# Up-projection loads counted as longer in the planner, and the down-projection's token blocks finished in turn

## The chip, the cores and the metric

One core of one Trainium2 chip. The metric is the device time of one execution, in microseconds (us); of the kernel before three executions were timed. One execution was profiled besides; all rows below are from it.

## What is computed

One decoder layer in float32 on 1024 tokens of width 1024 (token mixing, then a squared-ReLU MLP). The change touches the MLP only, the last line of the reference:

```python
h = rms_norm(x, g_ffn_norm[l])
x = x + jnp.square(jax.nn.relu(h @ w_up[l])) @ w_down[l]   # w_up 1024 x 4096, w_down 4096 x 1024
```

## The kernel before

**Recording and planning.** The kernel does not emit instructions directly. Every call records a node in a `Plan` (so all of them stand at line 268, and the profile tells them apart by the names of their tiles). `Plan.schedule` (line 340) then decides the order of the instructions on every engine by playing the program through with costs of its own (`cost`, line 292): whenever an engine is free it takes, of the nodes that are ready in this play, the one with the highest `prio`, and that order is issued. An engine executes its instructions in that order, so a wait of one holds up all that stand behind it. Two numbers matter here. `n.prio` (line 376) is the longest chain of work behind a node, less 0.03 per place in the recorded program, plus `plus`. `done` (line 454) is when the node's result is there for others; for a DMA it is

```python
line = max(t + .4, line) + n.bytes / .36e6
done = line + 1.75
```

**Precision.** Each float32 operand is split in two float32r tiles: ScalarE (ACT) copies the high part, VectorE (DVE) or GpSimd (POOL) subtracts it from the original for the low part (`split`, line 1455). `mm3` makes three TensorE (PE) matmuls of 128x512 for each product.

**Up-projection** (`up_raw` line 1444, `product` 1469, `pair` 1539): 16 pairs of 128-column blocks of `w_up`. For each pair a load of 1 MB on SP's queue fills a tile `wu` (three buffers in turn), eight ACT instructions scale it by the norm's gain, POOL makes sums of it (`s1` to `s4`), and seven products of 12 matmuls follow (a Strassen-Winograd form). Their operand `we` is split from `wu` or from an `s`; there are six buffers for it. The products go into PSUM banks `X`, `Z`, `W`. `Z` takes the product S1, is copied out to a tile `d` by ACT, and then has S4 added to it, so PE's first matmul of S4 (`Z<-B22h`) waits for that copy (`d<-Z`). DVE and POOL combine the results, and SP stores them to DRAM (`u_d`).

**Down-projection** (line 1640): eight chunks `c` of two pairs, each with seven parts `p`. A part reads `u_d` (`ur`, split to `uu`) and the rows of `w_down` (`wd`, combined by POOL to `T`, split to `we`), and makes 4 token blocks `j` x 2 pairs x 3 = 24 matmuls into four banks, one for each `j`. After each block's six matmuls DVE adds the bank to the output rows `y` (`tt(nc.vector, y, X[j], y, ALU.add)`, line 1674). Parts 0 to 3 accumulate in the same four banks `X`, so the next part's first matmul into a bank waits for the add of the part before; parts 4 and 5, and part 6, use banks `Z`. In the last chunk the adds of parts 3 to 6 are followed by stores to the output.

Of the kernel before, what the change touches and what calls it, by code (L numbers as in the profile page):

```python
# [150 lines left out]
class Plan:  # L151
# [73 lines left out]
    done = False  # L225
# [8 lines left out]
    def op(self, name, engine, method, a, kw):  # L234
        views = [("" if i else "out", v) for i, v in enumerate(a)] + list(kw.items())
        views = [(k, v) for k, v in views if isinstance(v, View)]
        preds, raw, touched = set(), set(), []
        for k, v in views:
            w = k in ("out", "accum_out")
            r0, r1, m = v.region()  # L240
            touched.append((v.base, w, r0, r1, m))
            assert v.base.pool.bases is not None, v.base.kw
            preds.add(v.base.node.k)
            for n, ow, o0, o1, om in v.base.seen:
                if (w or ow) and r0 < o1 and o0 < r1 and m & om:
                    preds.add(n.k)
                    if ow:
                        raw.add(n.k)
        out = views[0][1] if views else None
        if name == "PE":  # L250
            preds.update([n.k for n in out.base.nodes if n.engine == "PE"][-1:])
        last = self.last_pe if name == "PE" else None
        if (last is not None and last.out is out.base and len(last.do) < self.GROUP and method == "matmul" and
                all(p <= last.k for p in preds)):
            node = last
            preds.discard(node.k)
        else:
            node = self.node(name)
            node.out = out.base if out is not None else None
        node.preds |= preds  # L260
        node.raw |= raw
        node.preds.update(p.k for p in self.follow)
        if name == "PE":
            self.last_pe = node

        def real(x):
            return x.real() if isinstance(x, View) else x
        node.do.append(lambda: getattr(engine, method)(*[real(x) for x in a], **{k: real(x) for k, x in kw.items()}))  # L268
        for b, w, r0, r1, m in touched:
            if b not in node.bases:  # L270
                b.nodes.append(node)
                node.bases.append(b)
            if w:
                b.seen = [s for s in b.seen if not (r0 <= s[2] and s[3] <= r1 and s[4] & ~m == 0)]
            b.seen.append((node, w, r0, r1, m))
        busy, late, size = self.cost(name, method, a, kw, views)
        node.plus = self.plus
        node.late = node.busy + late
        node.busy += busy
        node.port = self.port  # L280
        node.bytes += size
        node.names = method + " " + " ".join(v.base.kw["name"] for _, v in views)
        return node
# [1 line left out]
    last_pe = None  # L285
    plus = 0.0
    follow = ()
    drag = 1.0
    LINK = .05
    GROUP = 1  # L290

# [48 lines left out]
    def schedule(self, weight=lambda n: -.03 * n.k, rings=True):  # L340
# [52 lines left out]
        while True:  # L393
            while stack:
                n = stack.pop()
# [29 lines left out]
            n = nodes[heapq.heappop(ready[e])[1]]  # L425
# [29 lines left out]
            done = t + hold + n.late  # L455
            if n.bytes:
                line = max(t + .4, line) + n.bytes / .36e6
                done = line + 1.75
                if e != "POOL":
                    landed.append(done + .05)  # L460
            end = max(end, done)
            order.append(n)
            for b in n.bases:
# [32 lines left out]
def trunk_layer(ctx, tc, x, g_mix_norm, w_in, g_q, g_k, pe_cmp, w_cmp1, b_cmp1, w_cmp2, b_cmp2,  # L496
                conv_w, g_out, w_o, g_ffn_norm, w_up, w_down, out):
    plan = Plan(tc)
# [16 lines left out]
    def tt(eng, o, a, b, op):  # L515
        eng.tensor_tensor(o, a, b, op=op)

    def copy_act(o, i, scale=1.0):
        nc.scalar.activation(o, i, AF.Copy, scale=scale)
# [376 lines left out]
    with ExitStack() as b2:  # L896
# [150 lines left out]
        def y_tile(shape, name):  # L1047
            return yp.tile(shape, F32, name=name, tag="y", bufs=6)
# [164 lines left out]
        for it, tb in [*enumerate(ORDER)][6:] + [*enumerate(ORDER)][:6]:  # L1213
# [3 lines left out]
            for nh in range(2):  # L1217
                n = slice(nh * 512, (nh + 1) * 512)
# [25 lines left out]
    with ExitStack() as c_:  # L1244
# [112 lines left out]
        done = []  # L1357
# [49 lines left out]
        def bank_p(name):  # L1407
            return psP.tile([P, 512], F32, name=name, tag="pt")
# [35 lines left out]
        def up_raw(q):  # L1444
            raw = (ex.tile([P, KD, 2 * P], F32, name="wu", tag="x") if q % 3 == 0 else
                   vp.tile([P, KD, 2 * P], F32, name="wu", tag=("vs", "vw")[q % 3 - 1]))
            nc.sync.dma_start(raw, wuv[:, :, q * 2 * P:(q + 1) * 2 * P])
            for k in range(KD):
                copy_act(raw[:, k], raw[:, k], scale=cols[:, G_FFN + k:G_FFN + k + 1])
            return {f"A{i + 1}{j + 1}": raw[:, 4 * j:4 * j + 4, i * P:(i + 1) * P] for i in range(2) for j in range(2)}  # L1450

        def w_unit():
            return [ew.tile([P, 512], F32R, name="we", tag=f"w{q}", bufs=6) for q in "hl"]

        def split(pair, raw, eng):
            hi, lo = pair
            copy_act(hi, raw)
            tt(eng, lo, raw, hi.bitcast(F32), ALU.subtract)
            return hi, lo
# [53 lines left out]
    def bank_1(name):  # L1513
        return psD.tile([P, 512], F32, name=name, tag="1", bufs=1)

    def temp(name):
        return eT.tile([P, 512], F32, name=name, tag="t", bufs=4)
# [102 lines left out]
    def down_raw(q):  # L1620
        raw = (vp.tile([P, 2, D], F32, name="wd", tag=("vs", "vw")[q % 2]) if q % 4 < 2 else
               eR.tile([P, 2, D], F32, name="wd", bufs=2))
        nc.sync.dma_start(raw, wdv[:, 2 * q:2 * q + 2])
        B = {f"B{j + 1}{n + 1}": raw[:, j, n * 512:(n + 1) * 512] for j in range(2) for n in range(2)}
        B["T3"], B["T2"] = [temp(n) for n in ("T3", "T2")]
        tt(nc.gpsimd, B["T3"], B["B22"], B["B12"], ALU.subtract)
        return B

    def down_comb(B, name):
        if name == "T2":  # L1630
            B["T1"] = B["B12"]
            tt(nc.gpsimd, B["T1"], B["B12"], B["B11"], ALU.subtract)
            tt(nc.gpsimd, B["T2"], B["B22"], B["T1"], ALU.subtract)
        if name == "T4":
            B["T4"] = B["T2"]
            tt(nc.gpsimd, B["T4"], B["B21"], B["T2"], ALU.subtract)
        return B[name]

    ACC = [(0, 0), (0, 1), (1, 1), (1, 0), (1, 1), (0, 1), (0, 0)]
    for c in range(NPAIR // CHUNK):  # L1640
        qs = range(c * CHUNK, (c + 1) * CHUNK)
        Bs = [down_raw(q) for q in qs]
        if c == 0:
            for tb in [th * 4 + j for th in TH for j in range(4)]:
                yacc[tb] = ey.tile([P, D], F32, name=f"y{tb}")
        X = [None] * 4
        for p in range(7):
            ops = []
            for i, q in enumerate(qs):
                if c == 0 and p < 2:  # L1650
                    both = (y_tile([P, 2, 512], "uf") if p else (yl, e1)[i].tile([P, 2, 512], F32, name="uf", tag="x")).bitcast(F32R)
                    u, ur = [both[:, 0], both[:, 1]], both[:, 1].bitcast(F32)
                else:
                    u = [eU.tile([P, 512], F32R, name="uu", tag=f"u{h}", bufs=10) for h in "hl"]
                    ur = eu.tile([P, 512], F32, name="ur", bufs=8)
                nc.sync.dma_start(ur, u_d[q][p])
                split(u, ur, nc.gpsimd if i else nc.vector)
                w = split(w_unit(), down_comb(Bs[i], WANT[p]), nc.vector if i else nc.gpsimd)
                ops.append((u, w))
            if c == 0 and p in (0, 1):  # L1660
                for tb in range(TH[p] * 4, TH[p] * 4 + 4):
                    nc.sync.dma_start(yacc[tb], x2_d[tb * P:(tb + 1) * P])
            ih, n = ACC[p]
            for j in range(4):
                if p == 0:
                    X[j] = bank_p("X") if j < 3 else bank_1("X")
                elif p in (4, 6):
                    X[j] = bank_d("Z") if j % 2 else bank_e("Z")
                t = slice(j * P, (j + 1) * P)
                for i, ((uh, ul), (wh, wl)) in enumerate(ops):  # L1670
                    mm3(X[j], uh[:, t], ul[:, t], wh, wl, i == 0 and p in (0, 4, 6), i == CHUNK - 1, skip_group_check=True)
                tb = TH[ih] * 4 + j
                y = yacc[tb][:, n * 512:(n + 1) * 512]
                tt(nc.vector, y, X[j], y, ALU.add)
                if c == NPAIR // CHUNK - 1 and p >= 3:
                    nc.sync.dma_start(out2d[tb * P:(tb + 1) * P, n * 512:(n + 1) * 512], y)
    plan.issue()
# [28 lines left out]
```

## Time and profile before

| | us |
|---|---|
| median of 3 executions (lowest, highest) | 1235.27 (1233.68, 1236.08) |
| the profiled execution's own time | 1237.24 |
| its span, first to last instruction | 1235.5 |
| PE busy in the span | 1206.5 (98%) |
| DVE, ACT, POOL busy | 933.4, 713.5, 702.5 |
| up-projection in steady state | about 640 to 880 |
| down-projection | about 919 to 1235 |

In the rows, times are us unless ns is written; a row of a timeline has its start, its length, engine, line, operation, output<-inputs, shapes, how often, and in brackets the idle time before it and what ended that. The ends of PE's matmuls are modelled and overlap the next one's start, so what a wait costs PE is read from the starts. SPq is SP's sequencer, the queue that issues the DMAs.

### The profile page before, as it was taken

The page shows a single profiled execution, that of the slowest core. Times are in us where ns is not written, and L with a number is a line of the kernel's source. Part 1 is how long each engine was busy: PE and PEld are TensorE (multiplying, and loading weights), DVE is VectorE, ACT ScalarE, POOL GpSimd, SP SyncE. Part 2 cuts the span into 40 slices and gives each one's busy share as a digit, 9 for nine tenths or more (in the row PEclk, how much of TensorE's full clock was granted, in tenths as well). Part 3 has the DMA queues.
Part 4 walks back from the last instruction along what each step waited for, and adds up shares of the span by engine and source line. Part 5 has one row for each costly group of instructions (what it writes and reads, how often), then busy time and mean ns, then how long its engine had stood idle before and what let it go on. Part 6 is the DMA issues. An engine that isn't in the chain of part 4 may idle for free.

```text
span 1235.5 us, 18345 instructions
## 1 busy us (share of the span) xinstructions
PE 1206.5 (98%) x5970; PEld 994.5 (80%) x5970; DVE 933.4 (76%) x1784; ACT 713.5 (58%) x1586; POOL 702.5 (57%) x629
## 2 busy tenths in 40 slices
PE   7999999999989999999999999999999999999998
PEld 6878977777878888888788888788887787888786
DVE  6968857683787889988875656566668998888874
ACT  7567855551678888778865555545345444444440
POOL 2544300011245545335878777777889999888860
PEclk9999999999999999999999999999999999999999
DMA  6265621263110100002235453534549544553413
GB/s 244 60 192 192 169 72 51 69 216 141 61 69 35 69 17 20 27 18 75 80 131 167 148 179 123 164 117 161 186 146 393 182 148 162 166 168 130 129 39 136
DMA packets 104215, 156.06 MB, mean 126 GB/s; under 512 B 20212, under 2 KB 58184, under 8 KB 104120
## 3 DMA queue, kind: packets, MB, share of 16 engines
q1 hardware_dynamic: 97976, 147.09, 35.8%
q10 hardware_dynamic: 5376, 5.24, 1.2%
q0 software_dynamic: 768, 2.56, 0.7%
q8 instruction: 47, 0.77, 0.2%
q14 instruction: 48, 0.39, 0.1%
HBM read 106.63 MB, written 48.23 MB: 125 GB/s over the span
## 4 chain that ended last, share of the span: by engine, by line
PE 80%; DVE 6%; DMA 4%; ACT 3%; issue 2%; POOL 1%; SPq 0%; DVEq 0%; ACTq 0%; POOLq 0%
PE X L268 24%; PE Z L268 16%; PE zX L268 5%; PE tp L268 5%; PE ot L268 4%; PE wa L268 4%; PE W L268 4%; PE zp L268 3%; PE wc L268 3%; DMA wu<-in_w_up_dram 3%; PE zZ L268 3%; PE zW L268 1%; DVE y L268 1%; DVE we L268 1%; PE hp L268 1%
## 5 line engine op out<-in xcount | busy, mean ns | idle before, releaser
L268 PE MATMUL X<-we,uu 128*128 128x512 f32 x720 | 179.5, 390 | 2.0 <-DVE y L268 1.8
L268 PEld LDWEIGHTS X<-we,uu 128*128 128x128 f32 x720 | 134.5, 188 | 32.2 <-ACT uu L268 3.0
L268 PE MATMUL Z<-we,uu 128*128 128x512 f32 x576 | 146.8, 391 | 0.4 <-DVE y L268 0.4
L268 ACT ACTIVATE uu<-ur 128x512 fp32r<-128x512 f32 x108 | 66.7, 630 | 123.6 <-PE X L268 58.1
L268 PEld LDWEIGHTS Z<-we,uu 128*128 128x128 f32 x576 | 107.3, 188 | 25.4 <-DVE y L268 2.2
L268 ACT ACTIVATE pt<-pt,nm 128x640 f32<-128x640 f32 (+7 forms) x128 | 93.9, 737 | 25.5 <-DVE nm L268 24.8
L268 PE MATMUL tp<-ident,pt 128*128 128x128 f32 x528 | 103.3, 273 | 1.3 <-DVE pl L268 1.0
L268 POOL TENSOR_TENSOR d<-d 128x512 f32<-128x512 f32 x64 | 98.1, 1553 | 10.2 <-DVE d L268 8.2
L268 ACT ACTIVATE ph<-tp 128x512 fp32r<-128x512 f32 (+1 forms) x148 | 82.1, 575 | 31.2 <-PE tp L268 28.8
L268 DVE TENSOR_TENSOR pl<-tp,ph 128x512 fp32r<-128x512 f32 (+1 forms) x148 | 94.7, 655 | 7.2 <-ACT ph L268 6.7
L268 DVE TENSOR_TENSOR y<-X,y 128x512 f32<-128x512 f32 x128 | 79.8, 681 | 13.9 <-PE X L268 13.1
L268 POOL TENSOR_TENSOR uu<-ur,uu 128x512 fp32r<-128x512 f32 x54 | 77.5, 1438 | 13.8 <-DVE y L268 8.7
L268 DVE TENSOR_TENSOR we<-s,we 128x512 fp32r<-128x512 f32 x42 | 39.4, 937 | 56.6 <-ACT we L268 27.0
L268 DVE TENSOR_TENSOR uu<-ur,uu 128x512 fp32r<-128x512 f32 x54 | 71.2, 1331 | 12.9 <-ACT uu L268 12.3
L268 PEld LDWEIGHTS tp<-ident,pt 128*128 128x128 f32 x528 | 68.6, 140 | 13.8 <-POOL pt L268 1.4
L268 DVE TENSOR_TENSOR y<-Z,y 128x512 f32<-128x512 f32 x96 | 61.3, 683 | 20.3 <-PE Z L268 20.3
L268 ACT ACTIVATE wu<-wu,cols 128x256 f32<-128x256 f32 x128 | 55.6, 500 | 24.0 <-DMA wu<-in_w_up_dram 23.1
L268 ACT ACTIVATE we<-wu 128x512 fp32r<-128x512 f32 x57 | 35.9, 631 | 57.5 <-PE X L268 48.6
L268 DVE SCALAR_TENSOR_TENSOR d<-d 128x512 f32<-128x512 f32 x48 | 68.2, 1423 | 0.8
L268 ACT ACTIVATE we<-s 128x512 fp32r<-128x512 f32 x55 | 34.4, 626 | 49.8 <-PE Z L268 30.2
L268 POOL IOTA d_sw<- 128x640 f32 (+1 forms) x2 | 1.2, 610 | 109.0 <-PE zZ L268 109.0
L268 PE MATMUL zp<-w_lo,hTh 128*128 128x512 f32 (+1 forms) x192 | 62.4, 365 | 0.1
(1334 smaller groups left out, 3714.4 us busy)
## 6 DMA issues: line engine op xcount, KB each, us to landing
u_d<-d SPq DMA_DIRECT2D x112, 256.0 KB, 4.1
ur<-u_d SPq DMA_DIRECT2D x108, 256.0 KB, 2.8
wu<-in_w_up_dram SPq DMA_DIRECT2D x16, 1024.0 KB, 5.5
wd<-in_w_down_dram SPq DMA_DIRECT2D x16, 1024.0 KB, 5.8
xt<-in_x_dram SPq DMA_DIRECT2D x10, 512.0 KB, 4.8
w_raw<-in_w_in_dram SPq DMA_DIRECT2D x8, 512.0 KB, 5.4
w_raw<-in_w_cmp_dram SPq DMA_DIRECT2D x16, 256.0 KB, 2.7
q_d<-qn SPq DMA_DIRECT2D x8, 512.0 KB, 3.4
```

The source lines that it names most:

```text
L268: node.do.append(lambda: getattr(engine, method)(*[real(x) for x in a], **{k: real(x) for k, x in kw.items()}))
```

## The change

Nodes get a number `slack`, which the play adds to `done` of a DMA. The loads of `w_up` for the pairs from 3 on get 5 us of it (`up_raw`); the other loads that are named get 0. In the down-projection the matmuls and the add of token block `j` get a `plus` of 0.7 x (3 - j). No instruction is added or removed, and none computes anything else.

```diff
--- before.py
+++ after.py
@@ -274,7 +274,7 @@
                 b.seen = [s for s in b.seen if not (r0 <= s[2] and s[3] <= r1 and s[4] & ~m == 0)]
             b.seen.append((node, w, r0, r1, m))
         busy, late, size = self.cost(name, method, a, kw, views)
-        node.plus = self.plus
+        node.plus, node.slack = self.plus, self.slack
         node.late = node.busy + late
         node.busy += busy
         node.port = self.port
@@ -285,7 +285,7 @@
     last_pe = None
     plus = 0.0
     follow = ()
-    drag = 1.0
+    drag, slack = 1.0, 0.0
     LINK = .05
     GROUP = 1
 
@@ -458,6 +458,7 @@
                 done = line + 1.75
                 if e != "POOL":
                     landed.append(done + .05)
+                done += n.slack
             end = max(end, done)
             order.append(n)
             for b in n.bases:
@@ -1444,7 +1445,9 @@
         def up_raw(q):
             raw = (ex.tile([P, KD, 2 * P], F32, name="wu", tag="x") if q % 3 == 0 else
                    vp.tile([P, KD, 2 * P], F32, name="wu", tag=("vs", "vw")[q % 3 - 1]))
+            plan.slack = 5.0 if q > 2 else 0.0
             nc.sync.dma_start(raw, wuv[:, :, q * 2 * P:(q + 1) * 2 * P])
+            plan.slack = 0.0
             for k in range(KD):
                 copy_act(raw[:, k], raw[:, k], scale=cols[:, G_FFN + k:G_FFN + k + 1])
             return {f"A{i + 1}{j + 1}": raw[:, 4 * j:4 * j + 4, i * P:(i + 1) * P] for i in range(2) for j in range(2)}
@@ -1620,7 +1623,9 @@
     def down_raw(q):
         raw = (vp.tile([P, 2, D], F32, name="wd", tag=("vs", "vw")[q % 2]) if q % 4 < 2 else
                eR.tile([P, 2, D], F32, name="wd", bufs=2))
+        plan.slack = float(0)
         nc.sync.dma_start(raw, wdv[:, 2 * q:2 * q + 2])
+        plan.slack = 0.0
         B = {f"B{j + 1}{n + 1}": raw[:, j, n * 512:(n + 1) * 512] for j in range(2) for n in range(2)}
         B["T3"], B["T2"] = [temp(n) for n in ("T3", "T2")]
         tt(nc.gpsimd, B["T3"], B["B22"], B["B12"], ALU.subtract)
@@ -1653,7 +1658,9 @@
                 else:
                     u = [eU.tile([P, 512], F32R, name="uu", tag=f"u{h}", bufs=10) for h in "hl"]
                     ur = eu.tile([P, 512], F32, name="ur", bufs=8)
+                plan.slack = 0.0
                 nc.sync.dma_start(ur, u_d[q][p])
+                plan.slack = 0.0
                 split(u, ur, nc.gpsimd if i else nc.vector)
                 w = split(w_unit(), down_comb(Bs[i], WANT[p]), nc.vector if i else nc.gpsimd)
                 ops.append((u, w))
@@ -1667,11 +1674,13 @@
                 elif p in (4, 6):
                     X[j] = bank_d("Z") if j % 2 else bank_e("Z")
                 t = slice(j * P, (j + 1) * P)
+                plan.plus = float(.7) * (3 - j) if True else 0.0
                 for i, ((uh, ul), (wh, wl)) in enumerate(ops):
                     mm3(X[j], uh[:, t], ul[:, t], wh, wl, i == 0 and p in (0, 4, 6), i == CHUNK - 1, skip_group_check=True)
                 tb = TH[ih] * 4 + j
                 y = yacc[tb][:, n * 512:(n + 1) * 512]
                 tt(nc.vector, y, X[j], y, ALU.add)
+                plan.plus = 0.0
                 if c == NPAIR // CHUNK - 1 and p >= 3:
                     nc.sync.dma_start(out2d[tb * P:(tb + 1) * P, n * 512:(n + 1) * 512], y)
     plan.issue()
```

**ACT, up-projection, the load `wu_8788`** (in the profiled execution the one issued at 770.50). `we` are high parts, `d` are results copied out of PSUM; `wu<-wu,cols` scales the load's pieces. Before:

```order
L268 ACTIVATE we_8821<-wu_8470 128x512
L268 ACTIVATE d_8675<-X_8468 128x512
L268 ACTIVATE wu_8788<-wu_8788,cols_64 128x256
L268 ACTIVATE we_8845<-s2_8715 128x512
L268 ACTIVATE d_8690<-Z_8613 128x512
L268 ACTIVATE wu_8788<-wu_8788,cols_64 128x256 x6
L268 ACTIVATE we_8877<-s1_8711 128x512
L268 ACTIVATE d_8840<-X_8654 128x512
L268 ACTIVATE we_8890<-s3_8752 128x512
L268 ACTIVATE wu_8788<-wu_8788,cols_64 128x256
L268 ACTIVATE we_8913<-s4_8773 128x512
```

Now:

```order
L268 ACTIVATE we_8821<-wu_8477 128x512
L268 ACTIVATE d_8671<-X_8468 128x512
L268 ACTIVATE we_8845<-s2_8709 128x512
L268 ACTIVATE d_8686<-Z_8612 128x512
L268 ACTIVATE we_8871<-s1_8703 128x512
L268 ACTIVATE d_8840<-X_8656 128x512
L268 ACTIVATE we_8883<-s3_8749 128x512
L268 ACTIVATE wu_8788<-wu_8788,cols_64 128x256 x7
L268 ACTIVATE we_8912<-s4_8773 128x512
L268 ACTIVATE wu_8788<-wu_8788,cols_64 128x256
```

All eight scalings of the load now stand behind the copy `d<-Z`, the copy `d<-X` and three high parts; before, one stood ahead of these and six more ahead of three of them.

**DVE, down-projection, end of part 0 of the sixth chunk.** `y` are the output rows, X the banks of the four token blocks; `uu` and `we` are low parts. Before:

```order
L268 TENSOR_TENSOR we_11908<-T3_11592,we_11918 128x512
L268 TENSOR_TENSOR uu_11946<-ur_11743,uu_11939 128x512
L268 TENSOR_TENSOR y0_10044<-X_11799,y0_10044 128x512
L268 TENSOR_TENSOR y1_10043<-X_11807,y1_10043 128x512
L268 TENSOR_TENSOR y2_10042<-X_11813,y2_10042 128x512
L268 TENSOR_TENSOR y3_10041<-X_11820,y3_10041 128x512
L268 TENSOR_TENSOR we_11962<-T2_11621,we_11968 128x512
```

Now:

```order
L268 TENSOR_TENSOR y2_10042<-Z_11852,y2_10042 128x512
L268 TENSOR_TENSOR y0_10044<-X_11750,y0_10044 128x512
L268 TENSOR_TENSOR y3_10041<-Z_11870,y3_10041 128x512
L268 TENSOR_TENSOR we_11923<-T3_11610,we_11931 128x512
L268 TENSOR_TENSOR y1_10043<-X_11773,y1_10043 128x512
L268 TENSOR_TENSOR y2_10042<-X_11806,y2_10042 128x512
L268 TENSOR_TENSOR y3_10041<-X_11825,y3_10041 128x512
L268 TENSOR_TENSOR uu_11953<-ur_11758,uu_11946 128x512
```

The add of block 0 has moved ahead of a low part, and the four adds stand no longer in one run.

**PE, the same place.** Before, from the last matmul of part 0 into block 0's bank, X_11799, to the next part's:

```order
L268 MATMUL X_11799<-we_11804,uu_11707 128x512
L268 MATMUL X_11813<-we_11795,uu_11701 128x512
L268 MATMUL X_11807<-we_11804,uu_11707 128x512
L268 MATMUL X_11820<-we_11795,uu_11701 128x512
L268 MATMUL X_11813<-we_11804,uu_11707 128x512
L268 MATMUL X_11820<-we_11804,uu_11707 128x512
L268 MATMUL X_11799<-we_11836,uu_11720 128x512
L268 MATMUL X_11799<-we_11826,uu_11720 128x512
```

Now, from the last matmul of part 0 into block 0's bank, X_11750; the next part's first into it is the fourth row below these:

```order
L268 MATMUL X_11750<-we_11812,uu_11707 128x512
L268 MATMUL X_11773<-we_11812,uu_11700 128x512
L268 MATMUL X_11806<-we_11775,uu_11681 128x512
L268 MATMUL Z_11870<-we_11783,uu_11652 128x512
L268 MATMUL X_11773<-we_11803,uu_11700 128x512
L268 MATMUL X_11806<-we_11787,uu_11688 128x512
L268 MATMUL X_11825<-we_11787,uu_11681 128x512
L268 MATMUL X_11773<-we_11812,uu_11707 128x512
L268 MATMUL X_11806<-we_11812,uu_11700 128x512
L268 MATMUL X_11825<-we_11775,uu_11681 128x512
L268 MATMUL X_11806<-we_11803,uu_11700 128x512
L268 MATMUL X_11825<-we_11787,uu_11688 128x512
```

From the last matmul into block 0's bank to the next part's first were 6 places and are 15; for block 1 they were 7 (X_11807) and are 12 (X_11773). Over the whole down-projection the shortest such distance was 5 (and 6 ten times), and is 12.

**PE, the end of the program.** The four banks Z are those of the last part's token blocks 0 to 3. Before, the last six matmuls:

```order
L268 MATMUL Z_12859<-we_12809,uu_12723 128x512
L268 MATMUL Z_12870<-we_12800,uu_12716 128x512
L268 MATMUL Z_12864<-we_12809,uu_12723 128x512
L268 MATMUL Z_12875<-we_12800,uu_12716 128x512
L268 MATMUL Z_12870<-we_12809,uu_12723 128x512
L268 MATMUL Z_12875<-we_12809,uu_12723 128x512
```

Now, the last ten:

```order
L268 MATMUL Z_12874<-we_12799,uu_12705 128x512
L268 MATMUL Z_12858<-we_12817,uu_12724 128x512
L268 MATMUL Z_12867<-we_12817,uu_12718 128x512
L268 MATMUL Z_12874<-we_12792,uu_12705 128x512
L268 MATMUL Z_12867<-we_12811,uu_12718 128x512
L268 MATMUL Z_12874<-we_12799,uu_12711 128x512
L268 MATMUL Z_12867<-we_12817,uu_12724 128x512
L268 MATMUL Z_12874<-we_12817,uu_12718 128x512
L268 MATMUL Z_12874<-we_12811,uu_12718 128x512
L268 MATMUL Z_12874<-we_12817,uu_12724 128x512
```

Before, the blocks ended 5, 3, 1 and 0 places ahead of the end. Now the third and the fourth end 3 and 0 places ahead of it, the second (Z_12858) 8, and the first (Z_12846, above these rows) 14.

## Rows read from the trace of the kernel before

**Rows 1.** Stretches: us, busy us of PE, PEld, DVE, ACT, POOL, clock, DMA share, GB/s.

```profile
640.00:880.00 240.00, 236.74 (x1037) 193.37 (x1036) 147.62 (x139) 126.25 (x248) 186.62 (x127) 1.00 0.46 155
...
940.00:1000.00 60.00, 58.97 (x259) 48.19 (x258) 57.24 (x68) 28.50 (x48) 56.59 (x39) 1.00 0.69 244
```

**Rows 2.** The chain that ended last: start, us, what.

```profile
654.00 6.14 DMA wu<-in_w_up_dram
...
731.80 6.05 DMA wu<-in_w_up_dram
...
770.50 7.94 DMA wu<-in_w_up_dram
...
849.66 6.05 DMA wu<-in_w_up_dram
...
920.56 7.35 DMA y<-x_d
...
1087.52 5.44 PE X L268 x24
```

**Rows 3.** Groups, PE and ACT, 640 to 880: xcount | busy, mean ns | idle before.

```profile
L268 PE MATMUL Z<-B22h,we 128*128 128x512 f32 x104 | 38.9, 396 | 3.3 <-ACT d L268 3.2
...
L268 ACT ACTIVATE wu<-wu,cols 128x256 f32<-128x256 f32 x96 | 41.1, 497 | 22.2 <-DMA wu<-in_w_up_dram 21.3 <-DVE d L268 0.8
```

**Rows 4.** Timeline of PE at 738 and at 777.

```profile
738.84 0.39 PE L268 MATMUL X<-T3h,we 128*128 128x512 f32 x1
739.50 0.50 PE L268 MATMUL Z<-B22h,we 128*128 128x512 f32 x1 [0.27 <-ACT d L268]
739.83 0.40 PE L268 MATMUL X<-B11h,we 128*128 128x512 f32 x1
...
777.53 0.39 PE L268 MATMUL X<-T3h,we 128*128 128x512 f32 x1
780.08 0.50 PE L268 MATMUL Z<-B22h,we 128*128 128x512 f32 x1 [2.16 <-ACT d L268]
```

**Rows 5.** Timelines of ACT and POOL, 778 to 808.

```profile
778.52 0.51 ACT L268 ACTIVATE wu<-wu,cols 128x256 f32<-128x256 f32 x1 [5.11 <-DMA wu<-in_w_up_dram]
...
779.45 0.58 ACT L268 ACTIVATE d<-Z 128x512 f32<-128x512 f32 x1
...
783.33 0.62 ACT L268 ACTIVATE we<-s 128x512 fp32r<-128x512 f32 x1
...
807.96 0.62 ACT L268 ACTIVATE we<-wu 128x512 fp32r<-128x512 f32 x1
...
788.43 1.30 POOL L268 TENSOR_TENSOR s<-wu,s 128x512 f32<-128x512 f32 x1 [0.69 <-DVE we L268]
```

**Rows 6.** Groups of PE's matmuls, 880 to 1236.

```profile
L268 PE MATMUL X<-we,uu 128*128 128x512 f32 x720 | 179.5, 390 | 2.0 <-DVE y L268 1.8
L268 PE MATMUL Z<-we,uu 128*128 128x512 f32 x576 | 146.8, 391 | 0.4 <-DVE y L268 0.4
L268 PE MATMUL X<-we,uf 128*128 128x512 f32 x48 | 11.6, 396 | 0.3 <-DVE y L268 0.3
```

**Rows 7.** Timelines of DVE and of PE around 1119.

```profile
1117.34 1.82 DVE L268 TENSOR_TENSOR uu<-ur,uu 128x512 fp32r<-128x512 f32 x1 [1.13 <-ACT uu L268]
1119.08 2.47 DVE L268 TENSOR_TENSOR y<-X,y 128x512 f32<-128x512 f32 x4
1121.48 0.68 DVE L268 TENSOR_TENSOR we<-T,we 128x512 fp32r<-128x512 f32 x1
...
1119.91 1.40 PE L268 MATMUL X<-we,uu 128*128 128x512 f32 x5 [0.40 <-DVE y L268]
```

**Rows 8.** Timelines of PE and of DVE at the end.

```profile
1220.17 10.28 PE L268 MATMUL Z<-we,uu 128*128 128x512 f32 x44
...
1229.35 2.48 DVE L268 TENSOR_TENSOR y<-Z,y 128x512 f32<-128x512 f32 x4 [3.10 <-PE Z L268]
```

**Rows 9.** Groups of DVE's instructions, 940 to 1236.

```profile
L268 DVE TENSOR_TENSOR uu<-ur,uu 128x512 fp32r<-128x512 f32 x52 | 69.9, 1356 | 12.9 <-ACT uu L268 12.3 <-issue 0.5
```

## The prediction

> **What bounds the kernel now.** Read first the stretches. From 640 to 880, the steady up-projection, PE is busy 236.74 of 240 us, and at 940 to 1000, early in the down-projection, 58.97 of 60 [rows 1]. So PE bounds both stages, and a change of order can win only the places where PE waits. The chain that ended last gives the pace where nothing is waited for: 24 matmuls in 5.44 us, 0.227 each [rows 2]. The chain also leaves PE for a load of `w_up` six times, every second pair, from 654.00 to 849.66; these loads take about 6.05 us, that of 770.50 took 7.94 [rows 2].
>
> What these loads do to PE is seen in the groups: ACT's scaling idles 21.3 us for them, and the first matmuls of the product S4 (`Z<-B22h`) idle 3.3 us for ACT's copy `d<-Z` [rows 3]. PE's timeline prices one such wait. After 738.84 the next matmul was due at 739.07 and began at 739.50: 0.43 lost, where the bracket says 0.27, because the modelled end of the matmul before lies 0.16 beyond its slot. The matmul behind it follows after 0.33 instead of 0.23, another 0.10. At 777.53 the same wait costs 2.55 - 0.23 = 2.32 [rows 4]. ACT's timeline shows why: it sat 5.11 us before `wu` at 778.52, and `d<-Z`, which needs nothing of that load, stood behind it and ran at 779.45 [rows 5].
>
> In the down-projection PE waits for DVE's adds: 2.0 us ahead of matmuls into X, 0.4 into Z, and 0.3 in the first parts (`uf`) [rows 6]. At 1119.91 it is the hand-off of block 0's bank: DVE spent 1.82 us on a low part and began the four adds only at 1119.08 [rows 7].
>
> **Up-projection: 4.9 us.** The change puts the eight scalings behind `d<-Z`, `d<-X` and three high parts, none of which needs the load. All six waits should go: 3.3 of idle, and 6 x (0.16 + 0.10) that the brackets leave out, 4.9 in all. PE's own order in the steady pairs is unchanged, and so is the place of the loads among SP's stores; a load is issued when a buffer of three comes free, which the change does not move. What becomes later is the scaling. If ACT starts it only after the third high part, at 783.95 by the old times, eight at 0.43 (41.1 / 96 [rows 3]) end at 787.4. The load's first high part is taken from it at 807.96, and POOL first has to finish the sums of the load before, the last of which ran to 789.73 [rows 5]. So some 2 us of cover are left for the sums and 20 for the high parts, and a load of 7.94 us instead of 6.05 is covered as well. Two sides: 4.9 is the whole of it; if one wait in three stays because of the reordered first pairs, 3.3.
>
> **Down-projection: 2.4 us.** Five waits of this kind (the X and Z groups) come to 2.4 of idle and 5 x 0.16, 3.2 us [rows 6]. The hand-off at 1119.91 had 6 places, 1.36 us, and lost 0.40 + 0.16, so it needed 1.92. Every hand-off now has at least 12 places, 2.72 us, and block 0's 15, 3.4. The add of block 0 stands ahead of the low parts that used to delay it. That leaves 0.8 us over, as much as one low part stretches (1.82 against a shortest of 0.68 [rows 7]) beyond its mean. The wait in the `uf` part stays: it hangs on the load of `y` from DRAM, 7.35 us [rows 2]. I count 2.4 of the 3.2, since at 940 to 1000 DVE (57.24) and POOL (56.59 of 60 us) are nearly full themselves [rows 1] and part of a wait may come back there. Bounds: 0 and 3.2.
>
> **End: 0.7 us.** The last matmul ends at 1230.45, the four adds run from 1229.35 to 1231.83 [rows 8]. Now the banks end 14, 8, 3 and 0 places before the end; three adds (0.62 each) lie beside PE and the fourth ends near 1231.15. The stores behind them move with it.
>
> **New waits: -0.6 us.** Nearly every down-projection matmul stands in another place, and the planner's costs are not the chip's. The old order had about one wait a chunk of 0.3 to 0.6 us; I leave one or two such, 0.6 in all. On the other side this is 0.
>
> Sum: 4.9 + 2.4 + 0.7 - 0.6 = 7.4 against the profiled execution's 1237.24, so 1229.8. That execution lies 1.97 above the median. Its slow load alone cost 2.32 - 0.43 = 1.89 more than the ordinary one. If the timed executions had no such load, the gain from 1235.27 is 5.5, and the result 1229.8; if they had it, 7.4 and 1227.9. I take the middle, 1228.8.
>
> **Rivals.**
>
> *The low parts come between the adds (15%).* DVE's adds now stand singly among low parts, which average 1.36 us [rows 9] and reach 1.82 [rows 7]. One such and an add of 0.62, with some 0.3 to start, make 2.74, just the 2.72 of 12 places: the down-projection then waits as before, elsewhere. Left are 4.9 + 0.7, less up to 1.9 for the slow load: 1229.7 to 1231.6. For it speaks the 1.82 at 1117.34; against it that block 0, with 15 places, sets the pace of a part.
> The Trainium skill (GPSIMD Engine Reference, Specifications) says that GpSimd shares its SBUF interfaces with VectorE and contends with VectorE instructions that have two SBUF inputs: by it the low parts stretch wherever POOL runs, and the adds, with one input in PSUM, do not; the time would be this rival's. The rows agree so far: low parts of one size took 0.68 and 1.82, the four adds 2.47 together.
>
> *The operand buffers come too late (5%, slower).* The six buffers of `we` are held longer, since the blocks of a part end one after the other. In the down-projection's order the shortest distance from a buffer's last use to the first use of what takes its place was 38 places (8.6 us) and is 33 (7.5 us). In it lie ACT's copy (0.62), POOL's subtraction, and whatever POOL has queued. POOL's instructions average 56.59 / 39 = 1.45 us at 940 to 1000 [rows 1]; with its own and four ahead of it, 0.6 + 5 x 1.45 = 7.9, the time is over. Then PE loses up to the 1.1 us of the 5 places in each of the 14 parts of the first two chunks, 15.4, which outweighs the 8.0 gained: 1235.3 + 7.4, about 1242.7. It decides from four queued instructions on. Against it: POOL still has 6% to spare there, and no wait of PE for POOL stands in the groups.
>
> *The up-projection's waits only change their cause (10%).* `d<-Z` no longer stands behind the load, but may stand behind a high part that waits for a free buffer, or the sums may run late after all. Then 2.4 + 0.7 or less is left: 1232.2 to 1235, half of it no change that a measurement can tell. Against it: in the pairs between, where the load had landed in time, the same copy makes PE wait nowhere; of 104 matmuls `Z<-B22h` only six places show it.
>
> **Chances and range.** 70% for the forecast, with 1226 to 1231 as its own range: 1225.9 is all of 4.9 + 3.2 + 0.7 with 0.6 of the `uf` wait, taken from the median. With the first rival, 85% lie below 1231.6. A measurement of this kernel tells about 0.2% (2.5 us) from no change. Faster by more: the forecast, the first rival and a third of the last, 0.88. Within it: 0.07. Slower: 0.05. The range runs from 1226.0 to 1232.5.
>
> **What would show it.** Right: on the chain no load of `w_up` after the third pair; in the group `Z<-B22h` no idle for ACT `d`; ACT's scaling idle for the load 0 to 5 us instead of 21.3; idle of X and Z for DVE `y` under 1 us; one add behind the last matmul. Wrong: PE idle for `we` or `uu` in the down-projection (second rival); DVE `y` idle of 2 us and more (first); PE waiting for `d` or `we` every second pair still (third).

## The result, and the profile after

Median of 6 executions 1225.2 us (1224.55 to 1226.32), beside it 1235.33 for the kernel before: 0.9919 of its time (95% interval 0.9906 to 0.9932), 10.1 us less. The direction is the one forecast; 1225.2 lies 0.8 below the range, and the gain is 10.1 where 6.5 was predicted. The profiled execution took 1224.93 us, its span is 1223.2.

The stretches of [rows 1], in the changed kernel:

```profile
640.00:880.00 240.00, 240.00 (x1059) 198.41 (x1059) 144.34 (x141) 132.45 (x258) 189.22 (x130) 1.00 0.47 156
...
940.00:1000.00 60.00, 60.00 (x267) 49.67 (x266) 54.63 (x69) 28.42 (x49) 57.07 (x39) 1.00 0.61 213
```

PE has no gap left in either, and 22 more matmuls fall into the first (1059 instead of 1037). The groups from 640 to 880 that answer to [rows 3]:

```profile
L268 ACT ACTIVATE wu<-wu,cols 128x256 f32<-128x256 f32 x104 | 44.5, 496 | 1.2 <-DMA wu<-in_w_up_dram 1.2
...
L268 PE MATMUL Z<-B22h,we 128*128 128x512 f32 x105 | 38.7, 390 | 0.0
```

ACT's scaling waits 1.2 us for loads instead of 21.3, and S4's first matmuls wait no more. ACT's timeline at the place of [rows 5] shows the order itself:

```profile
774.60 0.60 ACT L268 ACTIVATE d<-Z 128x512 f32<-128x512 f32 x1
777.55 0.63 ACT L268 ACTIVATE we<-s 128x512 fp32r<-128x512 f32 x1 [2.34 <-PE X L268]
778.27 0.60 ACT L268 ACTIVATE d<-X 128x512 f32<-128x512 f32 x1
778.91 0.64 ACT L268 ACTIVATE we<-s 128x512 fp32r<-128x512 f32 x1
779.45 2.89 ACT L268 ACTIVATE wu<-wu,cols 128x256 f32<-128x256 f32 x7
```

The copy of Z runs 4.9 us ahead of the first scaling, which finds its load landed. The chain that ended last holds no load of `w_up` after the third pair. For the down-projection, the groups from 880 on answer to [rows 6] and, with two more low parts in the stretch, to [rows 9]:

```profile
L268 PE MATMUL X<-we,uu 128*128 128x512 f32 x720 | 197.6, 389 | 0.0
L268 PE MATMUL Z<-we,uu 128*128 128x512 f32 x576 | 164.8, 389 | 0.0
...
L268 DVE TENSOR_TENSOR y<-X,y 128x512 f32<-128x512 f32 x128 | 85.2, 683 | 17.0 <-PE X L268 16.2
...
L268 DVE TENSOR_TENSOR y<-Z,y 128x512 f32<-128x512 f32 x96 | 65.1, 684 | 18.2 <-PE Z L268 17.8
L268 DVE TENSOR_TENSOR uu<-ur,uu 128x512 fp32r<-128x512 f32 x54 | 61.9, 1152 | 4.6 <-PE Z L268 3.3 <-ACT uu L268 1.3
...
L268 PE MATMUL X<-we,uf 128*128 128x512 f32 x48 | 11.3, 391 | 0.0
```

No matmul waits for an add, and here not for the load of `y` in the `uf` parts either. Now it is the adds that wait for PE (16.2 and 17.8 us). The hand-off of [rows 7], in DVE's timeline:

```profile
1106.88 0.69 DVE L268 TENSOR_TENSOR y<-X,y 128x512 f32<-128x512 f32 x1 [0.24 <-PE X L268]
1107.56 0.69 DVE L268 TENSOR_TENSOR y<-Z,y 128x512 f32<-128x512 f32 x1
1108.22 0.92 DVE L268 TENSOR_TENSOR we<-T,we 128x512 fp32r<-128x512 f32 x1
1109.07 1.28 DVE L268 TENSOR_TENSOR y<-X,y 128x512 f32<-128x512 f32 x2
```

Block 0's add begins when its bank is done, with no low part ahead of it, and PE goes on from 1107.36 without a gap. The end, for [rows 8]:

```profile
1213.67 5.38 PE L268 MATMUL Z<-we,uu 128*128 128x512 f32 x23
...
1218.40 1.37 DVE L268 TENSOR_TENSOR y<-Z,y 128x512 f32<-128x512 f32 x2 [0.44 <-PE Z L268]
```

PE ends at 1219.05 and the last add at 1219.77: one add behind it, 0.72 us instead of 1.38.

**PE's delay.** The brackets of a timeline turned out too small a measure (below), so the runs are compared by PE's starts. From each distance from one matmul's start to the next one's, the pace of 0.2267 us (24 matmuls in 5.44 us, [rows 2]) is taken off, and the rest is summed over a stretch. This is done for the 2582 to 2600 matmuls that begin from 632 us on. "Up-projection" is 632 to 919, "first parts" is 919 to 940. The delays are of one profiled execution each. The ratio is that of the times to those of the kernel before on the same chip. One execution with a slack of 10 took 2009.18 us at a mean granted clock of 0.559, where the others had 0.998 to 1.0, and its ratio leaves it out.

| kernel | ratio (95% interval) | up-projection | first parts | down, from 940 |
|---|---|---|---|---|
| before | | 5.6 | 1.0 | 5.3 |
| before, second profile | | 4.0 | 0.6 | 5.4 |
| slack only | 0.9975 (0.9965 to 0.9986) | 0.5 | 0.3 | 5.5 |
| plus only | 0.9952 (0.9940 to 0.9965) | 3.6 | 1.3 | 0.0 |
| the change | 0.9919 (0.9906 to 0.9932) | 0.4 | 0.0 | 0.0 |
| the change, second | 0.9918 (0.9897 to 0.9938) | 0.4 | 0.7 | 0.0 |
| the change, third | 0.9915 (0.9902 to 0.9928) | 0.5 | 0.5 | 0.0 |
| slack 2 instead of 5 | 0.9922 (0.9909 to 0.9936) | 0.3 | 1.5 | 0.0 |
| slack 10 | 0.9924 (0.9909 to 0.9938) | 0.5 | 0.0 | 0.0 |
| slack on all pairs | 0.9920 (0.9900 to 0.9940) | 0.3 | 1.5 | 0.0 |
| plus 0.2 instead of 0.7 | 0.9922 (0.9901 to 0.9942) | 0.6 | 0.2 | 1.4 |
| `y` in halves | 0.9931 (0.9911 to 0.9951) | 0.4 | 1.5 | 0.5 |
| `y` in halves, `ur` first | 0.9921 (0.9905 to 0.9937) | 0.4 | 0.0 | 0.0 |

### The profile page after: what moved, and what is told of

It is laid out like the page before. It is cut to its first block, busy times and chain, and to the rows that moved or that the text cites. A ratio compares the mean times of both kernels' runs of the same rounds, so it can differ in the third digit from the quotient of the medians.

```text
span 1223.2 us, 18339 instructions
## 1 busy us (share of the span) xinstructions
PE 1200.1 (98%) x5970; PEld 996.4 (81%) x5970; DVE 927.3 (76%) x1784; ACT 711.2 (58%) x1586; POOL 704.6 (58%) x629
## 4 chain that ended last, share of the span: by engine, by line
PE 86%; DVE 4%; ACT 3%; DMA 1%; issue 1%; POOL 1%; SPq 0%; ACTq 0%; DVEq 0%; POOLq 0%
PE X L268 28%; PE Z L268 18%; PE zX L268 5%; PE tp L268 5%; PE ot L268 4%; PE wa L268 4%; PE W L268 4%; PE zp L268 3%; PE wc L268 3%; PE zZ L268 3%; PE zW L268 1%; PE hp L268 1%; ACT ph L268 1%; DVE w_lo L268 1%; PE tpq L268 1%
## 5 line engine op out<-in xcount | busy, mean ns | idle before, releaser
L268 PE MATMUL X<-we,uu 128*128 128x512 f32 x720 | 197.6, 389 | 0.0
L268 PE MATMUL Z<-we,uu 128*128 128x512 f32 x576 | 164.8, 389 | 0.0
L268 DVE TENSOR_TENSOR y<-X,y 128x512 f32<-128x512 f32 x128 | 85.2, 683 | 17.0 <-PE X L268 16.2
L268 POOL TENSOR_TENSOR uu<-ur,uu 128x512 fp32r<-128x512 f32 x54 | 86.3, 1604 | 2.7 <-ACT uu L268 2.6
L268 DVE TENSOR_TENSOR y<-Z,y 128x512 f32<-128x512 f32 x96 | 65.1, 684 | 18.2 <-PE Z L268 17.8
L268 DVE TENSOR_TENSOR uu<-ur,uu 128x512 fp32r<-128x512 f32 x54 | 61.9, 1152 | 4.6 <-PE Z L268 3.3
L268 DVE TENSOR_TENSOR we<-wu,we 128x512 fp32r<-128x512 f32 x38 | 49.5, 1304 | 19.4 <-PE X L268 9.8
L268 POOL TENSOR_TENSOR pt<-pt,rr 128x640 f32<-128x640 f32 (+4 forms) x64 | 62.3, 1003 | 0.0
```

## The experiments

The edits are shown against the changed kernel.

### Each half of the change alone

```diff
-                plan.plus = float(.7) * (3 - j) if True else 0.0
+                plan.plus = 0.0
```

> Only the 5 us on the up-projection's loads; the plus of the token blocks is 0, so the down-projection has the order of the kernel before. Theory (the two parts' waits simply add up): between 632 and 880 us PE's starts lie behind the 0.227 us pace by under 0.4 us in all (before 5.6, after 0.3), and from 919 to the end by about 6.3, as before. The profiled execution of before had one load of 7.94 us that cost 1.89 more than an ordinary one; if the timed executions mostly have none, the gain is 5.3 - 1.9 = 3.4 and the time 1231.9; if they have it as often, 5.3 and 1230.0. Rival (the first part of the down-projection lost its 1.0 us because the up-projection ended earlier, not because of the plus): no wait near the first parts, 1230.9 or 1229.0. Second rival (the surplus over my sum came from the up-projection, which frees more than its six waits): 1228 or less.

```diff
-            plan.slack = 5.0 if q > 2 else 0.0
+            plan.slack = 0.0
```

> Only the plus of the token blocks; the loads of w_up count as before, so the up-projection has the order of the kernel before. Theory (the parts add up): PE lies behind its pace by 3.4 to 5.6 us between 632 and 880, the more the longer the loads take, with the six waits for ACT's copy of Z; from 919 to the end by under 0.3 (before 6.3); one add behind the last matmul. Gain 10.1 less that of the other part alone: 1235.3 - (5.3 down-projection + 1.0 first parts + 0.9 end = 7.2) = 1228.1, at least 1228.1 to 1229.0. Rival (the wait in the first parts hung on the load of y, which landed late by chance or because of the up-projection): that 1.0 stays, 1229.1 to 1230. Second rival (my sum was right in size for the down-projection, 2.4 + 0.7, and the rest of the gain is the up-projection's): 1232.

Measured: 1232.6 and 1230.24 us, where the kernel before took 1236.05; by the ratios the slack saves 3.1 us (1.7 to 4.3) and the plus 5.9 (4.3 to 7.4). Together that is 9.0, and the whole change saved 10.1: within the intervals the two add up. PE's waits from 632 on with the slack alone:

```profile
PE X L268 <- DVE y L268: 1.8, 3, 1.0
PE Z L268 <- DVE y L268: 0.4, 1, 0.4
```

and with the plus alone:

```profile
PE Z L268 <- ACT d L268: 1.5, 5, 0.3
PE Z L268 <- ACT uu L268: 0.2, 1, 0.2
```

Each half removes its own kind of wait and leaves the other's. The second rival of each falls: the larger part of the gain is the down-projection's. The first rival of the plus holds in part. PE still lost 1.3 us in the first parts with it, so the plus does not free these parts of waits, but only some 0.2 of this stands at an add that needs `y`; 0.9 stands at two matmuls into Z and the ones behind them. With the slack alone PE lost 0.3 in the first parts, with no wait that a bracket shows; whether that was the slack or chance, as its first rival asks, these runs can't tell.

### The kernel before, profiled a second time

> The kernel before, profiled a second time. Theory (the profiled execution of before lay 1.9 above the median because one load of w_up took 7.94 us): no load of w_up takes over 7 us, PE lies 3.5 to 4 us behind its pace between 632 and 880 instead of 5.6, and the profiled time is about 1235.3. The waits of the down-projection stand at the same places (near 965, 1033, 1081, 1120, 1159 by the first profile) with 5 to 6.3 us in all. Rival (which waits come is chance in the down-projection too): the sum from 919 on differs from 6.3 by over 1 us, and the places differ; above all the one in the first parts, which hung on a load of y that took 8.9 us from issue to landing, is there or not by chance.

It took 1235.52. Five loads are on the chain, all of 6.03 to 6.20 us; the first and the last:

```profile
693.15 6.11 DMA wu<-in_w_up_dram
...
848.28 6.03 DMA wu<-in_w_up_dram
```

The up-projection's delay is 4.0 and not 5.6: no load like that of 7.94 us in [rows 2] is on the chain here. In the down-projection the same five places wait again, with the same lengths to some 0.03 us (1.19 in both, at 963 here and at 965 before); there the delay belongs to the order. In the first parts it was 0.6 instead of 1.0. PE's timeline shows what brackets leave out:

```profile
963.20 2.78 PE L268 MATMUL X<-we,uu 128*128 128x512 f32 x11 [1.03 <-DVE y L268]
...
1104.82 3.12 PE L268 MATMUL Z<-we,uu 128*128 128x512 f32 x12
```

Eleven matmuls at the pace are 10 x 0.2267 + 0.39 = 2.66, twelve 2.88. So the matmuls behind the wait at 963.20 lost 0.12 us more. The row at 1104.82 has no bracket at all and yet lost 0.24: one matmul began 0.13 late and the next 0.08, which the modelled end of the one before (0.16 beyond its slot) covers.

### How much slack, and on which loads

```diff
-            plan.slack = 5.0 if q > 2 else 0.0
+            plan.slack = 2.0 if q > 2 else 0.0
```

> The changed kernel with 2 us in place of 5 on the loads of w_up. In the steady pairs ACT's scaling of every second load then begins right behind the copy of Z, but the copy of X and two or three high parts (s1, s3) stand behind the first scalings again, as before the change. Theory (only the copy of Z made PE wait, so only its place behind the scaling counted): the time of the changed kernel, 1225.2 within 0.7; PE's delay between 632 and 880 under 0.5 us; ACT's idle ahead of the scaling between 5 and 20 us. Rival (the 0.4 us more than the brackets showed, and what the load holds up besides, hang on the other instructions behind it): part of the six waits stays for d of X or for we, 1 us or more between 632 and 880, and 1226 to 1228.

```diff
-            plan.slack = 5.0 if q > 2 else 0.0
+            plan.slack = 10.0 if q > 2 else 0.0
```

> The changed kernel with 10 us on the loads of w_up: ACT's scaling now stands also behind the copy of X and more high parts, in every pair. Theory (the load has cover on both sides: POOL's sums begin late, but the first sum is needed only some 8 us later): PE's delay between 632 and 880 stays under 0.5 us and the time is that of the changed kernel within 0.7. Rival (2 us of cover were all that my prediction left for the sums; one more place or a slow load uses them up): PE waits for we or the sums in every second pair, 1 to 4 us between 632 and 880, and 1226.5 to 1229.5.

ACT's scaling from 640 to 880 with 2 us:

```profile
L268 ACT ACTIVATE wu<-wu,cols 128x256 f32<-128x256 f32 x97 | 40.9, 496 | 3.2 <-DMA wu<-in_w_up_dram 3.2
```

and with 10 us:

```profile
L268 ACT ACTIVATE wu<-wu,cols 128x256 f32<-128x256 f32 x104 | 45.5, 496 | 0.0
```

With 2 us the copy of Z, with the high part ahead of it, has moved ahead of the scaling; the copy of X has not, and PE's delay in the up-projection is 0.3. So the place of the copy of Z was enough. (ACT's idle of 3.2 is below the 5 to 20 I expected; the scaling begins late enough anyway.) With 10 us, the other side, it is 0.5: the sums still come in time. The ratios can't be told from that of the change.

```diff
-            plan.slack = 5.0 if q > 2 else 0.0
+            plan.slack = 5.0
```

> The changed kernel with the 5 us on all loads of w_up, also those of the first three pairs, whose scaling stands ahead of the first high parts near 590 us; PE has waits of 0.2 to 0.4 us there, four or five of them, for the high and low parts of wu. Theory (it is the same mistake of the play, a load counted as too short): some 0.5 to 1 us goes there, 1224.5. Rival (that stretch is an interleaving of the last attention block with the first products; the other order of 3189 rows of PE brings new waits, and these early loads have landed long before): the same or slower, 1225 to 1230.

The time (1226.40, the change beside it 1226.13) shows no gain, though it could not show one of 0.5 us. The waits speak for the rival: near 590 PE's two waits for ACT's `we` (0.6 us together) went, one of 0.8 for DVE's `t` came, and that for DVE's `we` grew from 0.3 to 0.7.

### A smaller plus

```diff
-                plan.plus = float(.7) * (3 - j) if True else 0.0
+                plan.plus = float(.2) * (3 - j) if True else 0.0
```

> The changed kernel with 0.2 x (3 - j) instead of 0.7 x (3 - j): the blocks end only partly in turn, and 25 hand-offs of a bank have 8 places or fewer (before the change 32, with it none; the shortest is 5 again). Theory (the down-projection's waits are those of short hand-offs, each paid with its idle time, the two late matmuls behind it and some 20 slower ones): from 940 on waits of 0.3 to 1.2 us stand at two to five of these hand-offs, 1 to 4 us in all, and the time is 1226 to 1229. Rival (it is enough that block 0 comes first; the number of places doesn't matter): under 0.4 us from 940 on, and the time of the changed kernel.

One hand-off waited, on DVE and PE:

```profile
1109.09 1.69 DVE L268 TENSOR_TENSOR uu<-ur,uu 128x512 fp32r<-128x512 f32 x1
1110.70 1.87 DVE L268 TENSOR_TENSOR y<-X,y 128x512 f32<-128x512 f32 x3
```

```profile
1111.43 1.90 PE L268 MATMUL X<-we,uu 128*128 128x512 f32 x7 [0.63 <-DVE y L268]
```

It has 8 places; a low part of 1.69 us stands ahead of the add. This is the pattern of [rows 7], and of my first rival. In the kernel before, all four waits for a bank X from 940 on stand at hand-offs of 6 places, and each of these four has a low part of 1.72 to 1.82 us right ahead of the add; the other six hand-offs of 6 places have none there and did not wait. In the three profiles of the change, with 12 places or more, none waited from 940 on. So the theory holds, with fewer waits than I thought (one; 1.4 us of delay): the 0.2 already removes most. It takes both to make a wait, the few places and the low part ahead. The plus changes both, the matmuls' turn and the add's place, and no run gave it to one of them alone. Its time (1226.53) can't be told from that of the change beside it (1226.13).

The Trainium skill (GPSIMD Engine Reference, Specifications) says that GpSimd contends for SBUF with VectorE instructions of two SBUF inputs. The rows agree: low parts are stretched still (1152 ns in the mean, shortest 0.68 us), the 224 adds, with one input in PSUM, are not (683 and 684). But that rule alone did not decide the time: in the changed kernel 12 of the 28 hand-offs of 12 places have a low part ahead of the add, of up to 1.83 us, and it fits in.

### The change again, and the first parts

> The changed kernel a second time, beside the three others. Theory (its waits from 632 us on are gone for good, except those of the first down-projection parts, where 4 MB of y and the ur behind them share some 400 GB/s and land by chance early or late): 1225.2 to 1226.2; PE under 0.3 us behind its pace from 632 to 919 and from 940 on, and 0 to 1.5 us between 919 and 940. Rival (the first profile was typical there too): under 0.1 us between 919 and 940.

> The changed kernel beside the two others, for a comparison on one chip: 0.9918 of the time of the kernel before; under 0.3 us of delay on PE from 632 on, except 0 to 1.5 us between 919 and 940.

The delays stay away in both long stretches in all three profiles of the change, and the first parts lost 0.7 and 0.5 us where the first profile lost nothing. Of the 0.4 to 0.5 left in the up-projection, where I had expected under 0.3, 0.2 are two single matmuls that began 0.11 late. In the second profile, on DVE and PE:

```profile
922.36 1.89 DVE L268 TENSOR_TENSOR y<-X,y 128x512 f32<-128x512 f32 x3 [0.63 <-DMA y<-x_d]
```

```profile
923.11 2.12 PE L268 MATMUL X<-we,uf 128*128 128x512 f32 x8 [0.33 <-DVE y L268]
```

That is the wait that I had left standing: the `y` of that add landed late. The trace tells the landing of two of the eight loads: 7.2 and 8.0 us after their issue in the first profile, 8.4 and 9.2 in this one. Two kernels try to take it away. First the loads of `y` in halves:

```diff
-            if c == 0 and p in (0, 1):
-                for tb in range(TH[p] * 4, TH[p] * 4 + 4):
-                    nc.sync.dma_start(yacc[tb], x2_d[tb * P:(tb + 1) * P])
             ih, n = ACC[p]
+            if c == 0 and p < 4:
+                for tb in range(TH[ih] * 4, TH[ih] * 4 + 4):
+                    nc.sync.dma_start(yacc[tb][:, n * 512:(n + 1) * 512], x2_d[tb * P:(tb + 1) * P, n * 512:(n + 1) * 512])
```

> The changed kernel with the loads of the output rows y cut in halves of 512 columns: part 0 asks for the left halves of its four rows, part 1 for the right ones, parts 2 and 3 for those of the other four. The same bytes, but only 1 MB stands ahead of part 0's adds instead of 2, and 1 MB less ahead of the ur of parts 2 to 6. Theory (the waits between 919 and 940, 0 to 1.5 us, hang on these transfers): no wait of DVE for the load of y and none of PE for y or uu there, the left halves land within 7 us, and the time is 0.3 to 1.0 us below the changed kernel beside it. Rival (twice as many DMA issues of 0.4 us each on SP hold back the ur behind them, and the order of the part is stirred up): a wait for uu or we of 0.5 us or more comes in their place, and the time is the same or up to 1 us longer.

PE waited for no add there any more (DVE itself still waited three times for `y`, 0.8 to 1.0 us, which I had not expected), and the wait moved: at 926.89 PE waited for ACT, which waited 4.97 us for `ur`.

```profile
926.89 0.50 PE L268 MATMUL X<-we,uu 128*128 128x512 f32 x1 [1.15 <-ACT uu L268]
```

On SP's queue the first two `ur` stood behind eight halves, and were issued 3.9 us after the first load instead of 1.8:

```profile
914.79 3.83 SPq L268 DMA_DIRECT2D y<-x_d  x8
918.66 1.10 SPq L268 DMA_DIRECT2D ur<-u_d  x2
```

That is the rival's mechanism. The time is 1227.97 beside 1226.13, more than the rival's 1 us, but the intervals of the two ratios overlap widely.

This kernel also waits where no other with the whole plus does, at 1079.77, on DVE and PE:

```profile
1075.80 1.50 DVE L268 TENSOR_TENSOR uu<-ur,uu 128x512 fp32r<-128x512 f32 x1
1077.23 1.80 DVE L268 TENSOR_TENSOR we<-T,we 128x512 fp32r<-128x512 f32 x1
1078.95 1.87 DVE L268 TENSOR_TENSOR y<-X,y 128x512 f32<-128x512 f32 x3
```

```profile
1079.77 2.55 PE L268 MATMUL X<-we,uu 128*128 128x512 f32 x10 [0.22 <-DVE y L268]
```

This hand-off has 14 places, 3.17 us, and two low parts, 3.3 us together, stand ahead of the add: my first rival, with the whole plus. The changed kernel has such a hand-off too, at 1001.05 in the first profile, with low parts of 1.28 and 1.78. There PE's matmul began 0.27 us behind the end of the add, where those that waited for an add began 0.06 to 0.15 behind it, so at most 0.2 us were to spare.

Then the same halves with a lower priority, all but the first four, so that the two `ur` pass them:

```diff
+            plan.plus = -4.0 if p else 0.0
             if c == 0 and p < 4:
...
+            plan.plus = 0.0
             for j in range(4):
```

> The halves of y once more, with a plus of -4 on all of them but part 0's left ones, so that the two ur of part 2 stand on SP ahead of the eight right halves of parts 1 and 2, not behind four of them. In the run before, the left halves came in time but these ur were issued 3.9 us after the first load instead of 1.8, and PE waited 1.3 us for uu. Theory (the wait is passed between the transfers by their order alone, so with both in time none is left): PE under 0.3 us behind its pace from 919 on, and 0.9910 of the time of the kernel before, some 1224.5 beside a changed kernel of 1225.5. Rival (SP lets only some nine transfers be under way, so whatever stands last of the 4.5 MB comes too late): a wait of 0.3 us or more stands at the right halves or at the ur of parts 3 to 6, and the time is that of the changed kernel.

```profile
915.10 1.74 SPq L268 DMA_DIRECT2D y<-x_d  x4
916.89 0.91 SPq L268 DMA_DIRECT2D ur<-u_d  x2
```

From 632 us on PE waits nowhere now, so the theory of the order holds in this one profile. The time doesn't show it: 1225.94, the change beside it 1225.04. A version that beats the change was not found.

## Why the size was wrong

**Up-projection, 4.9: right.** All six waits went, and only the copy's place behind the scaling mattered (slack 2). The six places and the matmuls right behind them lost 4.88 in the profile of before; the whole stretch gives 5.6 - 0.4 = 5.2. Of the 4.9 I discounted half of the slow load's 1.89. The two other profiles of the old order have no such load on the chain and lost 4.0 and, with the plus alone, 3.6, so the whole of it was rather an exception: 4.0 - 0.4 = 3.6 is the likely gain of a timed execution, and 3.1 (1.7 to 4.3) was measured.

One reading was wrong, without harm. The high part at 807.96 is taken from the load before the one of 770.50. By the tile numbers of the order this load is first read by POOL's sum at 801.13 and by ACT's high part at 809.74. So the cover for the sums was not 2 us but over 13, from 787.4 to 801.13, which fits that a slack of 10 costs nothing.

**Down-projection, "I count 2.4 of the 3.2": this step failed, and so did its bound.** The delay was 5.3 us, and all of it went. My 3.2 is what the five places lose by their own starts (3.18), but the price of a wait does not end there. Six matmuls behind these waits were late by 0.08 to 0.11 each, 0.54 in all, which I had counted for the up-projection and forgot here. Four more late places have no bracket, 0.75. And five to thirteen of the next matmuls behind such a place run at 229 to 260 ns, together with other small lags 0.86. That makes 5.33. Nor was there reason for the discount of 0.8: from 940 to 1000 POOL stayed as full as before (57.07 us, 56.59 in [rows 1]) and DVE nearly so (54.63, 57.24), yet no wait came back from 940 on in any kernel with the whole plus and whole loads of `y`.

The Trainium skill (Perfetto Trace Analysis, Identifying the Most-Contended Engine) warns that busy time of matmuls is no good measure of how close a kernel is to roofline, because they are pipelined. The trace agrees that it misleads: by busy time PE had 3.3 us to give from 640 to 880 [rows 1], by its starts 5.4.

**The `uf` wait "stays": right as a mechanism.** Its size is chance: the first parts lost 0.3 to 1.0 us in three profiles of the old order there and 0.0 to 0.7 in three of the change. That the first pair of profiles shows a gain of 1.0 there is luck of this pair.

**End, 0.7: right,** 0.66 by the adds, 0.2 more by the stores behind them.

**New waits, -0.6: wrong for the steady chunks.** None came with the change; with `y` in halves one did, 0.4 us. In the first parts they exist: with the plus alone, with slack 2 and with slack on all pairs PE lost 0.6 at two matmuls into Z between 930 and 939, of which the trace shows one waiting for `uu`.

**The sum.** From the second profile of before (1235.52) to the first of after (1224.93) are 10.6: 3.6 up-projection, 5.4 down-projection, 0.5 first parts, 0.9 end, and 0.2 of the stages ahead, which the change does not touch. Against my 4.0 (4.9 less half of 1.89) + 2.4 + 0.7 - 0.6 = 6.5 the down-projection alone is 3.0 more. The rest of the 4.1 are the 0.6 for new waits that did not come and, as luck, the 0.5 of the first parts; that the up-projection gave 0.4 less is made good by 0.2 at the end and 0.2 ahead.

**The rivals.** The low parts between the adds: seen with the plus at 0.2 and with `y` in halves, one wait each, not with the change, where the hand-off at 1001.05 had at most 0.2 us to spare. Operand buffers too late: with the change no matmul shows a wait for `we` from 632 on. The up-projection's waits changing their cause: refuted by the slack alone.

## What to carry to other kernels

Price a wait by the starts of the bounding engine over a whole stretch, against its undisturbed pace, not by the idle time in brackets: here that was 5.3 instead of 2.4. If one row of the profile is out of the ordinary, as the load of 7.94 us was, take a second profile before splitting the difference. A bank's hand-off wants so many places that all the instructions that may stand ahead of its release fit in: one low part did at 12 places, two of 3.3 us together did not at 14.

## What had not been expected

After a wait PE does not return to its pace at once: in the second profile of before, eleven matmuls behind one took 0.12 us too long, the first of them 80 ns late and most of the others 4 to 10 ns. What causes it was not tried.

In the first parts the DMA engines are full, 90% busy or more (a 9) in nearly every slice from 915.5 on. The view of the DMA gives, for the 40 slices of 912 to 932 us of the changed kernel,

```profile
DMA  6500007999989999999999999999999999999999
GB/s 238 209 0 0 0 0 246 344 377 393 401 328 320 393 401 410 393 389 389 418 434 410 426 410 442 401 401 401 434 401 369 393 393 385 393 389 365 389 422 410
```

The Trainium skill (DMA: Bandwidth & Descriptors, Where 436 GB/s comes from) gives 435 GB/s as the ceiling of the fabric, and some 358 as the limit of the HBM for one core, which by it binds transfers between HBM and SBUF. The measurement here goes beyond the 358 and decides: most slices from 916 on moved 365 to 442 GB/s, near the 435. A better order has little to win there, as far as the two kernels with halves show.

The stages ahead of the change vary more than the effects left over: the first matmul of the product `X<-T2h` after 600 us began between 621.87 and 624.43 us in the 13 profiles of all kernels. That is as wide as the 0.2% that a measurement of this kernel can't tell from no change.
